# Adaptive-norm decoder kernel: the first modulation vectors summed on TensorE with a held condition column

## The chip, the cores and the metric

The kernel runs on one core of one Trainium2 chip. A core has a matrix engine (TensorE, "PE" in the profile, with its weight loads listed apart as "PEld"), a vector engine (VectorE, "DVE"), a scalar engine (ScalarE, "ACT"), a general engine (GpSimd, "POOL") and SyncE ("SP"), which here only issues DMA transfers. Each engine works through its own instructions in the order in which the program gives them, and waits on semaphores for the others. The metric is device microseconds of one execution, the median of several runs.

## The reference

Two decoder layers over 256 tokens of width 2048, everything in float32: layer 0 mixes tokens by gated linear attention, layer 1 by softmax attention with a forget gate, and each has a gated MLP with a short convolution. What matters here is the conditioning. Every sub-layer's input is a normalised x, scaled and shifted by vectors that one matrix-vector product makes from the condition c:

```
cond = jax.nn.silu(c)
mod = (cond @ w_mod[i] + b_mod[i])[:, None, :]
sh_m, sc_m, g_m, sh_f, sc_f, g_f = jnp.split(mod, 6, axis=-1)
h = rmsnorm(x, norm_mix[i]) * (1.0 + sc_m) + sh_m
```

Each of the six pieces has 2048 entries, so each needs a 2048 x 2048 float32 block of `w_mod` (16 MB) that is used once. The first mixer of layer 0 cannot start before it has the parts of `sc_m` and `sh_m` that its first input rows need.

## The kernel before

A 2048-wide vector is held as 16 columns of 128 partitions (k-tiles); `cT` holds the condition so, one column for each k-tile. The first projection of layer 0 (`gla`, lines 669 to 709) runs over the first 8 k-tiles of h for all its output columns, and then over the other 8 (`BLOCKS = (8, 8)`, line 41). So at the start only the first 1024 entries of `sc_m` and of `sh_m` are needed: 2 x 2048 rows x 1024 columns, 16 MB. The rest of the modulation is computed later, in the background of the matmuls, by the same function `mod_tasks` (line 228) with smaller tiles.

At the start `queue_norm` (line 1202) makes 8 tasks for `sc_m` and then 8 for `sh_m`, each with one load of 1 MB on SP's queue (line 242; two k-tiles of 128 x 1024, into a slot of the pool `big`, which has 12 slots of 8 KB a partition). For the first four k-tiles (`DIRECT = 4`) TensorE multiplies: the weights are the stationary operand, 128 x 128 at a time, and one column of `cT` moves (line 257). For the other twelve VectorE multiplies a whole 128 x 1024 tile by one number for each partition and adds it to an accumulator (lines 261 and 263). What is then still to be summed over the 128 partitions is turned by eight TensorE transposes into PSUM (line 285) and reduced along the free axis by VectorE (line 289); bias, the TensorE part and, for `sc_m`, the norm's gain follow on VectorE (lines 297 to 302).

Between the first task and the others the kernel loads x (`load_x`, line 407: two loads of 1 MB behind the first four weight loads, 32 transposes, copies and squares on ScalarE, sums of squares on VectorE), sums the squares over the partitions by a matmul (line 458) and computes the reciprocal root (`token_rstd`, line 465). `make_h` (line 486) then makes h of one k-tile at a time: VectorE multiplies x by the root (line 500, `hn`), ScalarE applies scale and shift and rounds (line 501), VectorE makes the low part (lines 502 and 503). The projection's weight tiles are split into a rounded high part on ScalarE (line 115) and a low part on VectorE (line 119); the low parts of the first tiles stand behind h of the second k-tile by an explicit order (`gate`, lines 504 and 563 to 569). The first four projection tiles are loaded behind the last of the 16 weight loads (`after_startup`, line 221).

The order on each engine's queue is written when the kernel is built, by a planner that simulates the run and takes, at each engine, what is ready, in program order of priority; `issue_after` adds fixed orders. The order of the planner is not in the source.

Of the kernel before, what the change touches and what calls it, by code (L numbers as in the profile page):

```python
# [9 lines left out]
F32 = mybir.dt.float32  # L10
# [7 lines left out]
P = 128  # L18
# [11 lines left out]
SECT = {"sh_m": 0, "sc_m": 1, "g_m": 2, "sh_f": 3, "sc_f": 4, "g_f": 5}  # L30
RING = 7
AHEAD = 3
DIRECT = 4
XAFTER = 1
WIDE = 4
SLOAD = 12
BACK = 1
# [31 lines left out]
def kernel(  # L69
# [21 lines left out]
    def nm(s):  # L91
        cnt[0] += 1
        return f"{s}_{cnt[0]}"

    def bigt(shape, s="big"):
        return big.tile(shape, F32, tag="s8", name=nm(s))

    def ringt(shape, s="w"):
        return ring.tile(shape, F32, tag="w", name=nm(s))
# [22 lines left out]
    def misc():  # L122
        return psM.tile([P, 512], F32, tag="m" if PS[1] else "a", name=nm("pm"))
# [97 lines left out]
    def after_startup(on=True):  # L221
        es = ExitStack()
        if on and startup["left"] > 0 and len(startup["loads"]) >= BACK:
            startup["left"] -= 1
            es.enter_context(tc.issue_after(startup["loads"][-BACK]))
        return es

    def mod_tasks(l, key, f0=0, fn=D, wide=False, direct=0, defer=False):


        s = SECT[key]
        width = fn // -(-fn // 1024)
        per = 1
        while 2 * per * width <= (2048 if wide else 1024):
            per *= 2

        def chunk(c0, kt, st):
            def load():
                st[kt] = bigt([P, per, width], "wm") if wide else ringt([P, per, width], "wm")
                src = w_mod[l, kt * P:(kt + per) * P, s * D + c0:s * D + c0 + width]  # L240
                with after_startup(not wide):
                    dma = nc.sync.dma_start(out=st[kt], in_=src.rearrange("(k p) m -> p k m", p=P))
                if wide:
                    startup["loads"].append(dma.ins)

            def f():
                wt = st.pop(kt)
                m0, mn = c0 // P, width // P
                last = kt + per == KT
                if direct and kt == 0:  # L250
                    st["p"] = psA.tile([P, 512], F32, tag="a", name=nm("pd"))
                for j in range(per):
                    k = kt + j
                    col = cT[:, k:k + 1]
                    if k < direct:
                        for m in range(mn):
                            nc.tensor.matmul(st["p"][:, m:m + 1], wt[:, j, m * P:(m + 1) * P], col,
                                             start=(k == 0 and m == 0), stop=(k == direct - 1), skip_group_check=True)
                    elif k == direct:
                        st["a"] = accp.tile([P, 1024], F32, tag="acc", name=nm("acc"))[:, :width]  # L260
                        nc.vector.tensor_scalar(out=st["a"], in0=wt[:, j, :], scalar1=col, scalar2=None, op0=ALU.mult)
                    else:
                        nc.vector.scalar_tensor_tensor(out=st["a"], in0=wt[:, j, :], scalar=col, in1=st["a"],  # L263
                                                       op0=ALU.mult, op1=ALU.add)
                if last and defer:
                    deferred.append(finish)
                elif last and wide:
                    finish()
                elif last:
                    resting.append([REST, finish])  # L270

            def finish():
                m0, mn = c0 // P, width // P
                if defer:
                    pt = psA.tile([P, 512], F32, tag="a", name=nm("pt"))
                    for m in range(mn):
                        nc.tensor.matmul(pt[:, m:m + 1], st["a"][:, m * P:(m + 1) * P], one, start=(m == 0),
                                         stop=(m == mn - 1), skip_group_check=True)
                    red = pt
                else:  # L280
                    red = tmp.tile([P, 8], F32, tag="red", name=nm("red"))
                for q0 in range(0, 0 if defer else mn, 4):
                    pt = psA.tile([P, 512], F32, tag="a", name=nm("pt")) if wide else misc()
                    for m in range(min(4, mn - q0)):
                        nc.tensor.transpose(pt[:, m * P:(m + 1) * P], st["a"][:, (q0 + m) * P:(q0 + m + 1) * P],  # L285
                                            ident)
                    if wide:
                        mq = min(4, mn - q0)
                        nc.vector.tensor_reduce(out=red[:, q0:q0 + mq], in_=pt[:, :mq * P]
                                                .rearrange("p (m k) -> p m k", k=P), axis=AX.X, op=ALU.add)  # L290
                        continue
                    for m in range(min(4, mn - q0)):
                        blk = pt[:, m * P:(m + 1) * P]
                        nc.scalar.activation(blk, blk, AF.Copy, accum_out=red[:, q0 + m:q0 + m + 1])
                dst = mod[:, l * 6 + s, m0:m0 + mn]
                b0 = l * 96 + s * KT + m0
                nc.vector.tensor_tensor(out=dst, in0=red[:, :mn], in1=bm[:, b0:b0 + mn], op=ALU.add)
                if direct:
                    nc.vector.tensor_tensor(out=dst, in0=dst, in1=st["p"][:, :mn], op=ALU.add)
                if key[:2] == "sc":  # L300
                    gsrc = r0["nmix" if key == "sc_m" else "nffn"] + l * KT + m0
                    nc.vector.scalar_tensor_tensor(out=dst, in0=dst, scalar=1.0, in1=vec[:, gsrc:gsrc + mn],
                                                   op0=ALU.add, op1=ALU.mult)
                elif key[0] == "g":
                    nc.vector.tensor_scalar_add(dst, dst, 1.0)
            return load, f
        tasks = []
        for c0 in range(f0, f0 + fn, width):
            st = {}
            for kt in range(0, KT, per):  # L310
                tasks.append(chunk(c0, kt, st))
        return tasks
# [18 lines left out]
    def bg_step():  # L331
        prefetch(2)
        if pending:
            pending.popleft()()
# [868 lines left out]
        queue(mod_tasks(0, "sc_m", f0 * P, nb * P, *kind))  # L1203
        queue(mod_tasks(0, "sh_m", f0 * P, nb * P, *kind))

    def drain_startup():
        while bg or pending:
            prefetch(WIDE)
            bg_step()

    queue_norm(0, BLOCKS[0], True, DIRECT)
    for _ in range(XAFTER):
        prefetch(WIDE)
        bg_step()
    load_x()
    first_h = make_h(0, "m")
    drain_startup()
    bounds = [sum(BLOCKS[:i]) for i in range(len(BLOCKS))]

    def staged_h(m):  # L1220
# [87 lines left out]
```

## Time and profile before

| What | Value |
|---|---|
| Timed runs, median (lowest to highest of 3) | 2458.89 us (2458.03 to 2460.32) |
| Span of the profiled execution | 2463.1 us |
| PE busy | 2407.8 us, 98% |
| DVE busy | 1896.1 us, 77% |
| ACT busy | 1283.7 us, 52% |
| DMA, mean over the span | 259 GB/s, 78% busy |
| HBM read | 633.14 MB |

The profile is one execution, and a separate one from the timed runs; its own time is its span, 2463.1 us from the first instruction to the last, 4.2 us above the median of the timed runs. Busy shares are means over the whole run; the change touches only the first 60 us or so, so the parts of the profile that matter are those of that stretch. "L257" is line 257 of the kernel. A float32 matmul that is not of the rounded kind appears in the trace as two PE instructions. The ends of matmuls are modelled, so the pace of a row of matmuls is read from its starts: the time of the whole row divided by the number in it. PEclk is the clock that the throttle granted to TensorE, as a share of full speed.

### The profile page before, as it was taken

What the parts mean: (1) busy time and instruction counts of PE and PEld (TensorE: products, weight loads), DVE (VectorE), ACT (ScalarE), POOL (GpSimd) and SP (SyncE); (2) the same over time, 40 slices, a digit from 0 to 9 for tenths busy, and PEclk for the clock granted to TensorE, in tenths of its full rate; (3) what the DMA queues carried; (4) which work ended last, traced back from release to release, by engine and by line L of the source; (5) the groups of instructions that cost most, each with busy time, mean ns of one, the idle gap of its engine ahead of it and who ended that gap; (6) DMA issues with size and microseconds to landing.
All of it is one profiled execution on the core that took longest, in us unless ns stands there. A gap on an engine that the chain in (4) does not pass through costs nothing.

```text
span 2463.1 us, 47142 instructions
## 1 busy us (share of the span) xinstructions
PE 2407.8 (98%) x19190; PEld 2322.5 (94%) x19190; DVE 1896.1 (77%) x2508; ACT 1283.7 (52%) x1908; POOL 13.1 (1%) x35
## 2 busy tenths in 40 slices
PE   6999999899999999999999999999999999999998
PEld 6988899899999999999988888999999999999998
DVE  6776989877789999977587888887876777767544
ACT  2446555454656666543454555554655555565433
POOL 0000000000000000000000000000000000000000
PEclk7999999999999999999999999999999999999999
DMA  9897878898668899899589887687677777756553
GB/s 369 273 310 234 295 266 304 285 318 305 211 193 275 302 316 305 300 315 319 181 273 314 302 281 238 217 293 254 214 237 230 232 236 237 228 193 219 192 189 112
DMA packets 184310, 638.33 MB, mean 259 GB/s; under 512 B 23961, under 2 KB 24971, under 8 KB 183708
## 3 DMA queue, kind: packets, MB, share of 16 engines
q1 hardware_dynamic: 183128, 634.12, 77.4%
q8 instruction: 150, 2.46, 0.4%
q10 hardware_dynamic: 964, 1.20, 0.1%
q14 instruction: 68, 0.56, 0.1%
HBM read 633.14 MB, written 2.10 MB: 258 GB/s over the span
## 4 chain that ended last, share of the span: by engine, by line
PE 87%; DMA 6%; DVE 5%; issue 2%; ACT 1%; SPq 0%; DVEq 0%; ACTq 0%
PE pa L587 23%; PE pa L586 23%; PE pa L585 23%; DMA wm<-in_w_mod_dram 6%; PE pa L621 4%; PE pa L623 4%; PE pa L622 4%; DVE wl L119 2%; DVE acc L263 1%; PE pm L285 1%; PE pm L458 0%; PE pm L825 0%; PE pm L1036 0%; PE pm L847 0%; PE pm L982 0%
## 5 line engine op out<-in xcount | busy, mean ns | idle before, releaser
L115 ACT CAST wh<-w 128x1024 fp32r<-128x1024 f32 x819 | 855.9, 1048 | 949.1 <-PE pa L586 660.5
L119 DVE TENSOR_TENSOR wl<-w,wh 128x1024 fp32r<-128x1024 f32 x819 | 993.3, 1219 | 338.6 <-ACT wh L115 332.4
L585 PE MATMUL pa<-h,wh 128*128 128x256 f32 x3584 | 990.4, 278 | 6.7 <-ACT h L501 6.2
L587 PE MATMUL pa<-h,wl 128*128 128x256 f32 x3584 | 991.3, 278 | 4.4 <-DVE wl L119 4.4
L586 PE MATMUL pa<-h,wh 128*128 128x256 f32 x3584 | 993.1, 278 | 0.5 <-DVE h L503 0.2
L587 PEld LDWEIGHTS pa<-h,wl 128*128 128x128 f32 x3584 | 675.3, 189 | 7.5 <-DVE wl L119 5.1
L585 PEld LDWEIGHTS pa<-h,wh 128*128 128x128 f32 x3584 | 674.6, 189 | 7.8 <-ACT h L501 6.9
L586 PEld LDWEIGHTS pa<-h,wh 128*128 128x128 f32 x3584 | 676.9, 189 | 1.5 <-DVE h L503 1.3
L263 DVE SCALAR_TENSOR_TENSOR acc<-wm,cT,acc 128x1024 f32<-128x1024 f32 x352 | 451.2, 1282 | 144.8 <-DMA wm<-in_w_mod_dram 143.3
L586 PE MATMUL pa<-op,wh 128*128 128x256 f32 x1920 | 528.1, 276 | 0.3 <-DVE op L519 0.3
L585 PE MATMUL pa<-op,wh 128*128 128x256 f32 x1920 | 527.7, 276 | 0.4 <-DVE xT L644 0.4
L587 PE MATMUL pa<-op,wl 128*128 128x256 f32 x1920 | 524.7, 276 | 0.5 <-DVE wl L119 0.5
L586 PEld LDWEIGHTS pa<-op,wh 128*128 128x128 f32 x1920 | 360.4, 188 | 0.5 <-DVE op L519 0.5
L585 PEld LDWEIGHTS pa<-op,wh 128*128 128x128 f32 x1920 | 359.8, 188 | 0.6 <-DVE xT L644 0.6
L587 PEld LDWEIGHTS pa<-op,wl 128*128 128x128 f32 x1920 | 358.0, 188 | 0.9 <-DVE wl L119 0.9
L622 PE MATMUL pa<-wh,h 128*128 128x512 f32 x512 | 201.8, 395 | 0.0
L621 PE MATMUL pa<-wh,h 128*128 128x512 f32 x512 | 199.7, 394 | 0.0
L623 PE MATMUL pa<-wl,h 128*128 128x512 f32 x512 | 194.5, 394 | 0.0
L621 PEld LDWEIGHTS pa<-wh,h 128*128 128x128 f32 x512 | 96.8, 189 | 19.7 <-issue 0.2
L623 PEld LDWEIGHTS pa<-wl,h 128*128 128x128 f32 x512 | 96.5, 189 | 20.0 <-DVE wl L119 0.7
L622 PEld LDWEIGHTS pa<-wh,h 128*128 128x128 f32 x512 | 96.7, 189 | 19.4
L1088 ACT ACTIVATE y<-u,cw 128x256 f32<-128x256 f32 x176 | 101.6, 599 | 23.4 <-DVE act L1104 21.1
(250 smaller groups left out, 1365.4 us busy)
## 6 DMA issues: line engine op xcount, KB each, us to landing
wm<-in_w_mod_dram SPq DMA_DIRECT2D x352, 512.0 KB, 5.2
w<-in_ffn_w_up_dram SPq DMA_DIRECT2D x320, 512.0 KB, 4.5
w<-in_ffn_w_down_dram SPq DMA_DIRECT2D x176, 512.0 KB, 4.5
w<-in_fox_w_in_dram SPq DMA_DIRECT2D x128, 512.0 KB, 5.0
w<-in_gla_w_in_dram SPq DMA_DIRECT2D x96, 512.0 KB, 5.2
wm<-in_w_mod_dram SPq DMA_DIRECT2D x16, 1024.0 KB, 12.4
w<-in_gla_w_out_dram SPq DMA_DIRECT2D x32, 512.0 KB, 6.1
w<-in_ffn_w_up_dram SPq DMA_DIRECT2D x64, 256.0 KB, 4.0
```

Source lines behind the costliest of these rows:

```text
L115: nc.scalar.copy(out=hi, in_=src)
L119: order["v"] = nc.vector.tensor_tensor(out=lo, in0=src, in1=hi.bitcast(F32), op=ALU.subtract).ins
L263: nc.vector.scalar_tensor_tensor(out=st["a"], in0=wt[:, j, :], scalar=col, in1=st["a"], op0=ALU.mult, op1=ALU.add)
L285: nc.tensor.transpose(pt[:, m * P:(m + 1) * P], st["a"][:, (q0 + m) * P:(q0 + m + 1) * P], ident)
L585: nc.tensor.matmul(o, wh[:, ms], rh, start=(first and m % 2 == 0), stop=False, skip_group_check=True)
L586: nc.tensor.matmul(o, wh[:, ms], rl, start=False, stop=False, skip_group_check=True)
L587: nc.tensor.matmul(o, wl[:, ms], rh, start=False, stop=last, skip_group_check=True)
L621: nc.tensor.matmul(o, lh[:, ts_], wh[:, hs_], start=first, stop=False)
L622: nc.tensor.matmul(o, ll[:, ts_], wh[:, hs_], start=False, stop=False)
L623: nc.tensor.matmul(o, lh[:, ts_], wl[:, hs_], start=False, stop=last)
L1088: nc.scalar.activation(y, u, AF.Identity, scale=cw[:, l * 3 + 2, r:r + 1], bias=cw[:, 6 + l, r:r + 1])
```

## The change

The tasks of the first 16 MB leave `mod_tasks`, which loses its `wide` and `direct` ways. In their place:

- A tile `cz` (128 x 16 x 32) from the pool `big` is zeroed on GpSimd, and the condition columns are copied to its column 0 for each k-tile. A small tile `halfsel` (128 x 2) gets four ones: rows 0 and 64 in column 0, rows 32 and 96 in column 1.
- The loads are the same 16 of 1 MB, in the same order on SP, four ahead of x and then always four ahead of the sum that uses them.
- For each load TensorE does four float32 matmuls. Now `cz` of a k-tile is stationary (128 x 32, one real column) and 512 weight columns move past it. The four go to the four groups of 32 output partitions of one PSUM bank: groups 0 and 1 take the two halves of the first k-tile of the pair, groups 2 and 3 those of the second. All eight loads of `sc_m` (then of `sh_m`) accumulate in that bank, and rows 0, 32, 64 and 96 of it hold the result.
- `early_finish` copies the bank to SBUF on ScalarE, and four float32 matmuls turn it: 128 columns of the copy are stationary, `halfsel` moves, so that the two k-tile rows of each half are added and come out as columns. One VectorE instruction adds the bias; for `sc_m` a second one applies the gain.
- VectorE has no part in the sums of these 16 MB any more. The background sums of all later modulation are as before.

```diff
-    queue_norm(0, BLOCKS[0], True, DIRECT)
-    for _ in range(XAFTER):
-        prefetch(WIDE)
-        bg_step()
+    cz = bigt([P, KT, 32], "cz")
+    nc.gpsimd.memset(cz, 0.0)
+    nc.gpsimd.tensor_copy(out=cz[:, :, 0:1], in_=cT.rearrange("p (k o) -> p k o", o=1))
+    halfsel = const.tile([P, 2], F32, name="halfsel")
+    nc.gpsimd.memset(halfsel, 0.0)
+    for g in range(4):
+        nc.gpsimd.memset(halfsel[32 * g:32 * g + 1, g % 2:g % 2 + 1], 1.0)
+    early = {}
+
+    def early_load(key, j):
+        early[key, j] = wt = bigt([P, 2, 1024], "wm")
+        c0 = SECT[key] * D
+        src = w_mod[0, 2 * j * P:(2 * j + 2) * P, c0:c0 + 1024]
+        startup["loads"].append(nc.sync.dma_start(out=wt, in_=src.rearrange("(k p) m -> p k m", p=P)).ins)
+
+    def early_sum(key, j):
+        wt = early.pop((key, j))
+        if j == 0:
+            early[key] = psA.tile([P, 512], F32, tag="a", name=nm("pe"))
+        for g in range(4):
+            nc.tensor.matmul(early[key][32 * g:32 * g + 32, :], cz[:, 2 * j + g // 2, :],
+                             wt[:, g // 2, (g % 2) * 512:(g % 2 + 1) * 512], start=(j == 0), stop=(j == KT // 2 - 1),
+                             skip_group_check=True)
+
+    def early_finish(key):
+        rows_ = t2("er")
+        nc.scalar.copy(out=rows_, in_=early.pop(key))
+        pt = misc()
+        for b in range(4):
+            nc.tensor.matmul(pt[:, 2 * b:2 * b + 2], rows_[:, b * P:(b + 1) * P], halfsel, start=(b == 0),
+                             stop=(b == 3), skip_group_check=True)
+        dst = mod[:, SECT[key], 0:8]
+        b0 = SECT[key] * KT
+        nc.vector.tensor_tensor(out=dst.rearrange("p (h b) -> p h b", h=2),
+                                in0=pt[:, 0:8].rearrange("p (b h) -> p h b", h=2),
+                                in1=bm[:, b0:b0 + 8].rearrange("p (h b) -> p h b", h=2), op=ALU.add)
+        if key == "sc_m":
+            nc.vector.scalar_tensor_tensor(out=dst, in0=dst, scalar=1.0, in1=vec[:, r0["nmix"]:r0["nmix"] + 8],
+                                           op0=ALU.add, op1=ALU.mult)
+
+    todo = [(key, j) for key in ("sc_m", "sh_m") for j in range(KT // 2)]
+    for key_j in todo[:WIDE]:
+        early_load(*key_j)
     load_x()
     first_h = make_h(0, "m")
-    drain_startup()
+    for i, (key, j) in enumerate(todo):
+        if i + WIDE < len(todo):
+            early_load(*todo[i + WIDE])
+        early_sum(key, j)
+        if j == KT // 2 - 1:
+            early_finish(key)
```

More of the change, by code (lines that the diff above doesn't have):

```diff
@@ L226, in after_startup, with mod_tasks @@
         return es
-    def mod_tasks(l, key, f0=0, fn=D, wide=False, direct=0, defer=False):
+    def mod_tasks(l, key, f0=0, fn=D, defer=False):
         s = SECT[key]
@@ L233, in mod_tasks @@
         per = 1
-        while 2 * per * width <= (2048 if wide else 1024):
+        while 2 * per * width <= 1024:
             per *= 2
@@ L238, in load @@
             def load():
-                st[kt] = bigt([P, per, width], "wm") if wide else ringt([P, per, width], "wm")
+                st[kt] = ringt([P, per, width], "wm")
                 src = w_mod[l, kt * P:(kt + per) * P, s * D + c0:s * D + c0 + width]
[L241 to L244, printed above, removed]
+                with after_startup():
+                    nc.sync.dma_start(out=st[kt], in_=src.rearrange("(k p) m -> p k m", p=P))
             def f():
                 wt = st.pop(kt)
-                m0, mn = c0 // P, width // P
                 last = kt + per == KT
-                if direct and kt == 0:
-                    st["p"] = psA.tile([P, 512], F32, tag="a", name=nm("pd"))
                 for j in range(per):
@@ L254, in f @@
                     col = cT[:, k:k + 1]
[L255 to L259, printed above, removed]
+                    if k == 0:
                         st["a"] = accp.tile([P, 1024], F32, tag="acc", name=nm("acc"))[:, :width]
@@ L266, in f @@
                     deferred.append(finish)
-                elif last and wide:
-                    finish()
                 elif last:
@@ L274, in finish @@
                 if defer:
-                    pt = psA.tile([P, 512], F32, tag="a", name=nm("pt"))
+                    red = psA.tile([P, 512], F32, tag="a", name=nm("pt"))
                     for m in range(mn):
-                        nc.tensor.matmul(pt[:, m:m + 1], st["a"][:, m * P:(m + 1) * P], one, start=(m == 0),
+                        nc.tensor.matmul(red[:, m:m + 1], st["a"][:, m * P:(m + 1) * P], one, start=(m == 0),
                                          stop=(m == mn - 1), skip_group_check=True)
-                    red = pt
                 else:
@@ L282, in finish @@
                 for q0 in range(0, 0 if defer else mn, 4):
-                    pt = psA.tile([P, 512], F32, tag="a", name=nm("pt")) if wide else misc()
+                    pt = misc()
                     for m in range(min(4, mn - q0)):
@@ L286, in finish @@
                                             ident)
[L287 to L291, printed above, removed]
                     for m in range(min(4, mn - q0)):
@@ L297, in finish @@
                 nc.vector.tensor_tensor(out=dst, in0=red[:, :mn], in1=bm[:, b0:b0 + mn], op=ALU.add)
-                if direct:
-                    nc.vector.tensor_tensor(out=dst, in0=dst, in1=st["p"][:, :mn], op=ALU.add)
                 if key[:2] == "sc":
@@ new lines, in early_finish @@
+    def early_finish(key):
+        rows_ = t2("er")
+        nc.scalar.copy(out=rows_, in_=early.pop(key))
+        pt = misc()
+        for b in range(4):
[9 more added lines that the diff above has]
+                                           op0=ALU.add, op1=ALU.mult)
```

6 lines of the change are left out of this document (removed).

## The prediction

> **What bounds the kernel now.** I read the page first, then the busy time in two equal stretches, and then the chain of work that ended last, in order of time. (Columns of the stretches: stretch; length; busy time and instructions of PE, PEld, DVE, ACT, POOL; PEclk; DMA share; GB/s.)
>
> ```profile
> span 2463.1 us, 47142 instructions
> ...
> 0.00:61.60 61.60, 39.76 (x183) 37.15 (x184) 42.38 (x65) 14.91 (x24) 1.19 (x9) 0.78 0.93 369
> 61.60:123.20 61.60, 60.37 (x458) 57.89 (x458) 46.72 (x61) 30.06 (x38) 0.00 (x0) 0.95 0.83 273
> ```
>
> After the first 61.6 us TensorE hardly rests (60.4 of 61.6 us), and it goes on so to the end. So the start is a stretch ahead of a TensorE-bound kernel: one microsecond less until the first projection is one microsecond less at the end, as long as the work behind it moves along as a whole. It does: the next weight loads are released by the split of the first tiles, not by the clock on the wall.
>
> What ends the start is seen in the chain and in the timelines of the engines:
>
> ```profile
> 1.26 2.15 SPq L242 DMA_DIRECT2D wm<-in_w_mod_dram  x4
> 6.46 2.96 SPq L411 DMA_DIRECT2D xtok<-in_x_dram  x2
> ...
> 22.23 13.12 SPq L242 DMA_DIRECT2D wm<-in_w_mod_dram  x6
> 36.16 6.39 SPq L554 DMA_DIRECT2D w<-in_gla_w_in_dram  x4
> ```
>
> ```profile
> 42.00:51.00 9.00, 9.00 (x43) 8.82 (x42) 8.33 (x12) 0.47 (x1) 0.00 (x0) 0.50 1.03 409
> 59.50:64.60 5.10, 2.13 (x8) 1.84 (x8) 4.33 (x11) 3.99 (x7) 0.00 (x0) 0.50 0.01 2
> ```
>
> ```profile
> 52.19 5.23 DVE L263 SCALAR_TENSOR_TENSOR acc<-wm,cT,acc 128x1024 f32<-128x1024 f32 x4
> 52.81 1.04 ACT L115 CAST wh<-w 128x1024 fp32r<-128x1024 f32 x1 [9.53 <-DMA w<-in_gla_w_in_dram]
> 54.09 1.04 ACT L115 CAST wh<-w 128x1024 fp32r<-128x1024 f32 x1 [0.23 <-DMA w<-in_gla_w_in_dram]
> 57.48 1.97 PE L285 MATMUL pt<-ident,acc 128*128 128x128 f32 x8 [5.96 <-DVE acc L263]
> 59.48 0.69 DVE L289 TENSOR_REDUCE red<-pt 128x4 f32<-128x512 f32 x1 [0.16 <-PE pt L285]
> 60.21 0.17 DVE L297 TENSOR_TENSOR mod<-red,bm 128x8 f32<-128x8 f32 x1
> 60.61 1.58 ACT L501 ACTIVATE h<-hn,mod 128x256 fp32r<-128x256 f32 x3 [5.47 <-DVE mod L299]
> 64.62 0.58 PE L587 MATMUL pa<-h,wl 128*128 128x256 f32 x1 [1.23 <-DVE wl L119]
> ```
>
> The DMA engines are full (409 GB/s), so 1 MB (1.049 million bytes) takes 2.56 us. The order on SP is 4 weight loads, x, 12 weight loads, then the projection's tiles of 0.5 MB. The first of these had landed when its cast began, at 52.81. Half a megabyte is 1.28 us, so the sixteenth load landed at about 52.8 - 1.3 = 51.5. That is the floor of this start. VectorE is behind it: it runs four sums in a row until 57.42, then come transposes, reduction and bias, and h starts at 60.61. So there are 9.1 us between the last landing and h, 5.9 of them VectorE's backlog, 3.2 the turn.
>
> **The change, part by part.** *Removed*: VectorE's 24 passes and TensorE's 32 matmuls with one moving column. *Unchanged*: the sixteen loads, their order, x between them, and so the floor of 51.5. One slot of the pool is taken by `cz`, so 11 instead of 12 are left. The last loads were issued at 35 and landed 16 us later. An issue that comes a few us late is still in time; without that lead every late us would be one us. x's sums are in before 42.81 now, their root at 49.7:
>
> ```profile
> 42.81 0.47 ACT L467 ACTIVATE rb<-pm,epsc 128x256 f32<-128x256 f32 x1 [9.22 <-PE pm L458]
> 49.31 0.42 DVE L474 SCALAR_TENSOR_TENSOR rb<-ra,rb 128x256 f32<-128x256 f32 x1
> ```
>
> These 6.9 us are a few short operations with VectorE's sums between them; without the sums they shorten, so x has some 8 us to spare. `cz` and `halfsel` are small GpSimd fills, on an engine that does nothing there.
>
> *Added, a sum.* Each load brings four float32 matmuls, eight PE instructions, 512 columns each. For their price I take the projection's gate, which has the same form with fewer rows, and for the clock a row of transposes before and after the throttle let go:
>
> ```profile
> 228.89 1.98 PE L724 MATMUL pm<-wg,aT 17*128 17x512 f32 x4
> 21.43 1.07 PE L416 MATMUL pm<-ident,xtok 128*128 128x128 f32 x4
> 28.79 1.14 PE L416 MATMUL pm<-ident,xtok 128*128 128x128 f32 x8 [0.82 <-ACT xT L418]
> ```
>
> Four transposes took as long as eight did later, so full clock is twice half clock (PEclk reads 1.00 in both places, since it shows no event before 27.2; I go by the pace). Four gate instructions in 1.98 us, of which the last one's tail is some 0.2, start about 0.43 apart at full clock, so 0.86 at half. Eight in series would be 3.4 or 6.9 us for a load that arrives every 2.56: TensorE would become the bound. Side by side in four column groups they are two passes, 0.9 or 1.7 us, and the DMA stays the bound. No row here has four groups, but the scores of the gated attention go to two groups of 64. The loop (lines 817 to 826) issues all 16 instructions of one block of rows, then all of the next:
>
> ```profile
> 292.44 0.69 PE L825 MATMUL pm<-q,kend 128*64 128x64 f32 x9
> 292.91 0.27 PE L825 MATMUL pm<-q,k 128*64 128x64 f32 x1
> 292.97 0.22 PE L825 MATMUL pm<-q,kend 128*64 128x64 f32 x1
> 293.02 0.22 PE L825 MATMUL pm<-q,k 128*64 128x64 f32 x1
> 293.02 0.22 PE L825 MATMUL pm<-q,kend 128*64 128x64 f32 x1
> 293.08 0.22 PE L825 MATMUL pm<-q,k 128*64 128x64 f32 x1
> 293.08 0.22 PE L825 MATMUL pm<-q,kend 128*64 128x64 f32 x1
> ```
>
> Nine in one group start (0.69 - 0.22)/8 = 0.059 apart. Where the second block begins (`q,k` at 292.91) both groups run at that pace at once, and the new group starts while three older instructions of the other are still to start. With such a look-ahead all four groups of the change should be open together. I take two passes for the sum; the upper end is eight.
>
> The Trainium skill, "TensorE: Matmul & The Clock Gate", Part 3, says the reverse on the order: matmuls are strictly first in, first out, in start and in end. By that rule the second pass of each group would hold the next group back, a load would take five passes instead of two, and the result is the second rival below. The rows at 292.9 speak against it: a younger matmul starts before three older ones.
>
> *The clock.*
>
> ```profile
> 23.80:27.20 3.40, 3.38 (x15) 2.75 (x16) 3.36 (x4) 2.26 (x5) 0.00 (x0) 1.00 1.02 408
> 34.00:37.40 3.40, 2.15 (x11) 2.15 (x11) 3.30 (x5) 0.00 (x0) 0.23 (x2) 0.50 1.03 411
> 64.70:68.10 3.40, 3.40 (x16) 3.40 (x17) 3.40 (x5) 0.92 (x2) 0.00 (x0) 0.50 0.70 202
> 133.00:136.40 3.40, 1.46 (x7) 0.88 (x5) 0.94 (x1) 2.30 (x4) 0.00 (x0) 1.00 1.00 369
> 136.40:139.80 3.40, 3.00 (x11) 2.76 (x12) 3.40 (x5) 1.36 (x9) 0.00 (x0) 0.50 0.67 230
> ```
>
> A stretch of 3.4 us with PE busy for 1.46 was followed by half clock, one busy throughout by full clock. The sums keep PE busy for about 1.0 of 2.56 us at full clock (39%, like 1.46 of 3.4) and 1.8 (70%) at half. So I take half clock at the end of the start, as now. The same page, Part 1, asks only that no gap between bursts exceeds some 3 us; by that the clock would stay up, and h would come as in the second rival. The row at 133 speaks against: no gap there was that long, and the clock fell.
>
> *Added, the finish.* Copy of 128 x 512 out of PSUM; eight PE instructions with 128-column weights and two moving columns; one addition (0.17, as L297).
>
> ```profile
> 22.53 0.59 ACT L418 COPY xT<-pm 128x512 f32<-128x512 f32 x1 [16.22 <-PE pm L416]
> 36.80 4.82 PEld L257 LDWEIGHTS pd<-cT,wm 128*128 128x128 f32 x22
> ```
>
> Copy 0.6; turn 8 x 0.22 = 1.8, with its tail 1.9; addition with its hand-over 0.2.
>
> *A wait that is new.* The copy stands on ScalarE, where the casts of the first two projection tiles run from 52.81 and from 54.09. The planner writes the order. If only the first is ahead of the copy, the copy starts at 53.85; if both are, at 55.13. Nothing in the trace tells which (it has no such copy), so I take the middle. Behind the copy wait the turn, the addition, h and the whole projection.
>
> *The sum.* Landing 51.5; two passes and tail 2.0, to 53.5; copy at 53.85 or 55.13, done 54.45 or 55.7; turn to 56.35 or 57.6; addition to 56.55 or 57.8. Against 60.61 that is 4.0 or 2.8 us; the middle is 3.4. What follows h (the first low parts on VectorE, 64.62 - 60.61 = 4.0 us until TensorE is fed) keeps its order. In the profiled execution 2463.1 - 3.4 = 2459.7; against the median, 2458.9 - 3.4 = 2455.5. The 15 us of VectorE that fall away in the second half of the start were hidden or were this backlog; nothing else is worth time.
>
> **The rivals.** 1: *The four groups run in series.* Then TensorE decides, from the point where a sum takes over 2.56 us: fewer than 1.35 groups at once at full clock. 16 x 3.4 = 55 us from 7, with 2 us more for the first sums at half clock and some 5 for x's transposes and sums: about 69, copy 0.6, turn 0.9 and addition 0.2 at full clock, h at 70.7, 10 later than now; the first projection tile at full clock gives 2 back. 2458.9 + 8 = 2467. For it: no row has a 32-wide group or four at once. Against it: the rows at 292.9.
>
> 2: *Full clock at the end of the start*, by partial overlap that keeps TensorE busy. With five passes, a load takes 2.15 of 2.56 us (84%) and the clock stays up; with two passes it could be raised by a busy stretch. The end of the sum moves by little (51.5 + 2.4 = 53.9 in the first case), the turn shrinks by 0.9, and the projection starts at full clock. Now it runs from 64.62 to 68.2 at half pace, which costs 1.8. With a copy at 53.9 to 55.1: h at 55.6 to 56.9, 3.7 to 5.0 earlier, and 1.8 on top: 5.5 to 6.8, so about 2452.8. For it: the stretch from 23.8 to 27.2, busy for 3.38 of 3.40 with x's transposes, did lift the clock. Against it: 70% is well short of that.
>
> 3: *The gain does not arrive.* The planner puts the sum over x's squares behind the late sums on TensorE's queue (in the old trace it already waits for 22 one-column matmuls), or late slots open a hole in the DMA queue. If the square sum is behind the sixteenth sum, it starts at 53.5, and root and `hn` need about 4.5 more (42.81 to 49.31 now, with sums in between): h at 58 to 60. Time 2457 to 2459.
>
> **How the numbers follow.** Less than 0.2% (4.9 us) can't be told from no change here. Forecast (gain 2.8 to 4.0, half clock) 0.48; rival 2 0.27; rival 3 0.13; rival 1, with other losses of its kind, 0.12. Rival 2 is above that, and so is 0.04 of the forecast, if the hand-overs are shorter than I take them: faster 0.31. The rest of the forecast (0.44) and rival 3 are the same, 0.57; slower 0.12. The forecast's own range is 2454.5 to 2457. The range reaches to rival 2 with the lower end of its copy and to rival 3 with a small loss: 2451 to 2461; rival 1 is left out.
>
> **What would show it.** Two passes: PE matmuls into the new bank start in pairs of groups or all four within 0.2 us, and a load's eight take about 1.9 us. The floor: the cast of the first projection tile still starts near 52.8; if it comes later, slots were late. The finish: copy between 53.6 and 55.2, h between 56 and 58 instead of 60.61. The clock: half until some 3.5 us after the projection starts, else rival 2. The prediction is wrong if the last sum ends later than 56, or if the stretch from h on changes its length by more than 2 us.

## The result, and the profile after

The changed kernel takes 2542.89 us (median of 4 runs, 2542.28 to 2544.96), the kernel before, beside it on the same chip, 2459.61 us (2458.03 to 2462.13). The ratio is 1.0334, with a 95% interval of 1.0322 to 1.0346: slower by 3.3%, 83 us more. The profiled execution has a span of 2543.2 us.

The start did what was forecast. The timeline of the changed kernel around the last sums (start, length, engine, line, operation, number of instructions, idle time before it; L1205 is the new sum, L1211 the copy, L1214 the turn, L480 h, L566 the projection's low part, L587 before):

```profile
46.37 1.94 PE L1205 MATMUL pe<-wm,cz 128*32 128x512 f32 x8 [0.62 <-DMA wm<-in_w_mod_dram]
48.93 1.74 PE L1205 MATMUL pe<-wm,cz 128*32 128x512 f32 x8 [0.62 <-DMA wm<-in_w_mod_dram]
51.49 1.06 PE L1205 MATMUL pe<-wm,cz 128*32 128x512 f32 x8 [0.82 <-DMA wm<-in_w_mod_dram]
52.74 1.04 ACT L113 CAST wh<-w 128x1024 fp32r<-128x1024 f32 x1 [15.95 <-DMA w<-in_gla_w_in_dram]
53.70 0.58 ACT L1211 COPY er<-pe 128x512 f32<-128x512 f32 x1
54.17 1.05 ACT L113 CAST wh<-w 128x1024 fp32r<-128x1024 f32 x1
54.33 1.87 PE L1214 MATMUL pm<-halfsel,er 128*128 128x2 f32 x8 [1.77 <-ACT er L1211]
56.23 0.17 DVE L1218 TENSOR_TENSOR mod<-pm,bm 128x8 f32<-128x8 f32 x1 [15.69 <-PE pm L1214]
56.43 1.58 ACT L480 ACTIVATE h<-hn,mod 128x256 fp32r<-128x256 f32 x3 [1.21 <-DVE mod L1218]
60.45 0.58 PE L566 MATMUL pa<-h,wl 128*128 128x256 f32 x1 [1.23 <-DVE wl L117]
```

h starts at 56.43, 4.2 us ahead of the 60.61 of before, and the first low part at 60.45 instead of 64.62. So the loss is all behind this place: from h to the end it is 2463.1 - 60.61 = 2402.5 us before and 2543.2 - 56.43 = 2486.8 after, 84.3 more.

There the work is the same, but slower. The page of the changed kernel (busy time; chain of work that ended last; the largest groups, with busy time and mean ns of one; a 512-column group, from the groups by line):

```profile
span 2543.2 us, 47116 instructions
...
PE 2495.0 (98%) x19190; PEld 2384.0 (94%) x19190; DVE 1875.1 (74%) x2478; ACT 1286.2 (51%) x1910; POOL 14.1 (1%) x42
...
PE 96%; DMA 2%; DVE 1%; ACT 0%; issue 0%; SPq 0%; DVEq 0%
...
L564 PE MATMUL pa<-h,wh 128*128 128x256 f32 x3584 | 1011.1, 284 | 5.4 <-ACT h L480 5.3
...
L564 PE MATMUL pa<-op,wh 128*128 128x256 f32 x1920 | 538.9, 282 | 0.0
...
L601 PE MATMUL pa<-wh,h 128*128 128x512 f32 x512 | 204.3, 400 | 0.0
```

The same lines of the kernel before (L585 there is L564 here, L622 is L601):

```profile
PE 87%; DMA 6%; DVE 5%; issue 2%; ACT 1%; SPq 0%; DVEq 0%; ACTq 0%
...
L585 PE MATMUL pa<-h,wh 128*128 128x256 f32 x3584 | 990.4, 278 | 6.7 <-ACT h L501 6.2
...
L585 PE MATMUL pa<-op,wh 128*128 128x256 f32 x1920 | 527.7, 276 | 0.4 <-DVE xT L644 0.4
...
L622 PE MATMUL pa<-wh,h 128*128 128x512 f32 x512 | 201.8, 395 | 0.0
```

Each matmul is about 6 ns longer, with the same operands and shape. Ends are modelled, so the pace is better read from starts. A stretch of 50 us in the middle of both, first before, then after (after the length: busy time and number of PE, PEld, DVE, ACT, POOL; clock; DMA share; GB/s):

```profile
2000.00:2050.00 50.00, 50.00 (x443) 50.00 (x443) 37.28 (x49) 27.23 (x36) 0.00 (x0) 1.00 0.75 236
```

```profile
2000.00:2050.00 50.00, 50.00 (x422) 50.00 (x422) 29.97 (x39) 31.23 (x59) 0.00 (x0) 1.00 0.68 221
```

TensorE never rests in either, the clock is full in both, but 422 matmuls fit where 443 did: 118.5 instead of 112.9 ns each, about 5% slower. From start to start over the whole trace, the 256-column matmuls of the rounded kind went from 113.4 to 119.1 ns, the 512-column ones from 227.4 to 233.4. Each of the three products has 3584 + 1920 of the first and 512 of the second: 16,512 x 5.7 ns = 94 us and 1,536 x 6.0 ns = 9 us, 103 us together. The net loss behind h is 84 us. Part of the other 19 is found in the two traces: from h to the end TensorE is idle for 26.3 us instead of 34.1, and busy at half clock for 24.1 us instead of 37.0, which is worth some 6 us. A slower TensorE waits less (the chain of before ran over DMA and DVE for 6% and 5%, that of after for 2% and 1%); the half clock is partly chance, since an execution of the kernel before with one unused constant added (the first experiment below) has 24.9 us of it at the old pace. Some 5 us stay unexplained. The plain float32 matmuls, two instructions each, kept their pace (215 ns for 256 columns, 109 for 128, in both).

### The profile page after: what moved, and what is told of

Its sections match the earlier page's. It is cut to its first block, busy times and chain, and to the rows that moved or that the text cites. A ratio compares the mean times of both kernels' runs of the same rounds, so it can differ in the third digit from the quotient of the medians.

```text
span 2543.2 us, 47116 instructions
## 1 busy us (share of the span) xinstructions
PE 2495.0 (98%) x19190; PEld 2384.0 (94%) x19190; DVE 1875.1 (74%) x2478; ACT 1286.2 (51%) x1910; POOL 14.1 (1%) x42
## 4 chain that ended last, share of the span: by engine, by line
PE 96%; DMA 2%; DVE 1%; ACT 0%; issue 0%; SPq 0%; DVEq 0%
PE pa L565 26%; PE pa L566 26%; PE pa L564 26%; PE pa L600 5%; PE pa L601 5%; PE pa L602 5%; DMA wm<-in_w_mod_dram 1%; DMA w<-in_gla_w_in_dram 1%; PE pm L271 1%; DMA xtok<-in_x_dram 0%; PE pm L804 0%; PE pm L1015 0%; PE pm L826 0%; PE pm L961 0%; PE pm L979 0%; PE pm L437 0%
## 5 line engine op out<-in xcount | busy, mean ns | idle before, releaser
L564 PE MATMUL pa<-h,wh 128*128 128x256 f32 x3584 | 1011.1, 284 | 5.4 <-ACT h L480 5.3
L565 PE MATMUL pa<-h,wh 128*128 128x256 f32 x3584 | 1015.5, 284 | 0.8 <-DVE h L482 0.6
L566 PE MATMUL pa<-h,wl 128*128 128x256 f32 x3584 | 1011.9, 284 | 1.2 <-DVE wl L117 1.2
L564 PEld LDWEIGHTS pa<-h,wh 128*128 128x128 f32 x3584 | 680.3, 190 | 6.2 <-ACT h L480 5.6
L566 PEld LDWEIGHTS pa<-h,wl 128*128 128x128 f32 x3584 | 680.5, 190 | 4.1 <-issue 2.3
L565 PE MATMUL pa<-op,wh 128*128 128x256 f32 x1920 | 540.2, 282 | 0.0
L564 PE MATMUL pa<-op,wh 128*128 128x256 f32 x1920 | 538.9, 282 | 0.0
L566 PE MATMUL pa<-op,wl 128*128 128x256 f32 x1920 | 535.5, 282 | 0.0
L252 DVE SCALAR_TENSOR_TENSOR acc<-wm,cT,acc 128x1024 f32<-128x1024 f32 x330 | 422.7, 1281 | 104.5 <-DMA wm<-in_w_mod_dram 103.3
L564 PEld LDWEIGHTS pa<-op,wh 128*128 128x128 f32 x1920 | 363.1, 189 | 0.0
L566 PEld LDWEIGHTS pa<-op,wl 128*128 128x128 f32 x1920 | 361.0, 189 | 0.0
L601 PE MATMUL pa<-wh,h 128*128 128x512 f32 x512 | 204.3, 400 | 0.0
L600 PE MATMUL pa<-wh,h 128*128 128x512 f32 x512 | 202.3, 399 | 0.0
L601 PEld LDWEIGHTS pa<-wh,h 128*128 128x128 f32 x512 | 96.7, 189 | 21.9
```

The costliest lines, as they stand in the source:

```text
L564: nc.tensor.matmul(o, wh[:, ms], rh, start=(first and m % 2 == 0), stop=False, skip_group_check=True)
L565: nc.tensor.matmul(o, wh[:, ms], rl, start=False, stop=False, skip_group_check=True)
L566: nc.tensor.matmul(o, wl[:, ms], rh, start=False, stop=last, skip_group_check=True)
L600: nc.tensor.matmul(o, lh[:, ts_], wh[:, hs_], start=first, stop=False)
L601: nc.tensor.matmul(o, ll[:, ts_], wh[:, hs_], start=False, stop=False)
```

## The experiments

What could slow every rounded matmul by 6 ns, when the change ends at 57 us? It puts one small constant (`halfsel`, 32 bytes a partition) ahead of all later tiles, so that everything behind it lies 32 bytes higher. And it takes away the early use of another small tile: `red` (line 281, two slots, 64 bytes a partition), which `finish` took at the start in the kernel before. The addresses of the two programs show that the pools place a kind of tile where it is first taken. In the kernel before, `red` came ahead of the split weight tiles `wh` and `wl`; in the changed one they come first, 64 bytes lower. The addresses in the two programs, bytes a partition:

```
          big (h)      wh       wl      red    wh+64 - big   wl+192 - big
before     53952   178112   195520   178048   124224         141760
after      53984   178080   195488   214432   124160         141696
```

The 64 and 192 are `HELD = (16, 48)`, columns by which `split_w` (line 112) shifts a stationary high and low part inside its tile. The slots are steps of 4352 = 17 x 256, the parts of h lie multiples of 1024 apart, so a distance from the moving h to the loaded weights, modulo 256, holds for nearly all pairs: 64 (high) and 192 (low) before, 0 and 128 after. In the 512-column matmuls, where the weights move, h is loaded and `HELD` is not used, the distance from the moving weights to h is 0 before and 64 after. Theory A is that the absolute place counts, theory D that this distance does; the expectations below name the others.

**The constant alone, and the change without it.** To the kernel before a constant of the same size is added, and nothing reads it:

```diff
     xT = const.tile([P, KT, T], F32, name="xT")
+    shim = const.tile([P, 2], F32, name="shim")
+    nc.gpsimd.memset(shim, 0.0)
```

> The kernel before, with one unused constant of 8 bytes a partition put behind the last constant (it takes 32 bytes), and nothing else. Theory A, the place in SBUF: the changed kernel's small constant moved every tile that TensorE reads for the projections from a multiple of 64 bytes to 32 bytes past one, and each rounded matmul pays some 5 ns for that. Then this kernel is as slow behind the start: matmuls with 256 columns start 118 to 119 ns apart instead of 113, and the time is 2459.6 + about 87 = 2545 to 2549 us. Theory B, the 32-wide column groups leave TensorE in a slower way of working: no such group here, so 113 ns and 2459.6 us. Theory C, the program's length or instruction order: 2459.6 us, since TensorE's instructions are the same.

In the changed kernel, `halfsel` moves into spare columns of `cz`:

```diff
-    cz = bigt([P, KT, 32], "cz")
+    czt = bigt([P, KT * 32 + 2], "cz")
+    cz = czt[:, :KT * 32].rearrange("p (k o) -> p k o", o=32)
-    halfsel = const.tile([P, 2], F32, name="halfsel")
+    halfsel = czt[:, KT * 32:KT * 32 + 2]
```

> The changed kernel with its two selection columns kept behind the condition columns in the same pool slot, so that no constant is added and the tiles stand at multiples of 64 bytes again. Theory A: 113 ns a matmul, and the start of the changed kernel (h at 56.4 instead of 60.6): 2459.6 - 4.2 = 2455.4 us, between 2453.5 and 2457. Theories B and C: 118 to 119 ns, 2543 us as the changed kernel.

Measured: the constant costs nothing, 2460.08 us, ratio 1.0 (0.9989 to 1.0011); without it the change is as slow, 2540.8 us, 1.0327 (1.031 to 1.0344). The same stretch, first with the constant, then without it:

```profile
2000.00:2050.00 50.00, 50.00 (x444) 50.00 (x442) 37.04 (x48) 27.29 (x37) 0.00 (x0) 1.00 0.75 233
```

```profile
2000.00:2050.00 50.00, 50.00 (x422) 50.00 (x421) 33.04 (x41) 29.62 (x54) 0.00 (x0) 1.00 0.67 211
```

Theory A falls twice. In the first all tiles moved together and the pace stayed; in the second all tiles are back at multiples of 64, yet the weights are still 64 bytes closer to h, as `red` is still missing ahead of them.

**The distance alone, in the kernel before.** Nothing of the change; only `HELD`:

```diff
-HELD = (16, 48)
+HELD = (24, 56)
```

> The kernel before with the stationary weight tiles alone moved on by 32 bytes (offsets 24 and 56 columns instead of 16 and 48); h, the moving operand, stays at a multiple of 64. Theory A1, a moving row off the 64-byte grid costs one more line: 113 ns, 2459.6 us. Theory A2, a stationary tile off the grid costs it: 118 to 119 ns for the 256-column matmuls, unchanged 227 ns for the 512-column ones (these use no offset), about 2459.6 + 16500 x 5.3 ns = 2547 us less a little.

and with the constant of above and the weights 32 bytes lower:

```diff
-HELD = (16, 48)
+HELD = (8, 40)
```

> The kernel before with the 8-byte constant of the first run and the weight offsets set back by 32 bytes (8 and 40 columns), so that the stationary weights of the 256-column matmuls are at multiples of 64 and their moving operand h is 32 past. Theory A1 (moving): 118 to 119 ns, 2545 to 2549 us. Theory A2 (stationary): 113 ns for the 256-column matmuls, 232 for the 512-column ones, where both are off; 2459.6 + 1536 x 5.8 ns = 2468 us.

2520.19 us (ratio 1.0245, 1.022 to 1.0271) and 2528.34 us (1.0278, 1.0254 to 1.0303). Eight columns of shift in either direction cost 60 to 70 us. Theory A1 gave the first run 113 ns and theory A2 the second; both ran at about 118, so both fall. Neither run gives the full loss, so two more go to exactly the distance of the changed kernel, one by the weights alone:

```diff
-HELD = (16, 48)
+HELD = (0, 32)
```

> The kernel before with one constant changed: weight offsets 0 and 32 columns instead of 16 and 48, so the stationary weights stand 64 bytes lower and nothing else moves, which is what the change did to the 256-column matmuls. Theory D: 119 ns for the 256-column matmuls, 227 for the 512-column ones: what the changed kernel lost, less the 512-column matmuls' share of 9 us, so 2459.6 + 87 - 9 = about 2537 us. Theory B, or any theory that needs the column groups: 2459.6 us.

the other with h, and all behind it, 64 bytes higher, and the weights held where they were by the same `HELD`:

```diff
-HELD = (16, 48)
+HELD = (0, 32)
...
+    gapp = ctx.enter_context(tc.tile_pool(name="gapp", bufs=1))
     big = ctx.enter_context(tc.tile_pool(name="big", bufs=NBIG))
...
+    nc.gpsimd.memset(gapp.tile([P, 16], F32, name="gap"), 0.0)
```

> The kernel before with 64 bytes put between the pool of the raw weights and the pool that holds h, and the weight offsets lowered by 64 bytes (0 and 32 columns): the stationary weights keep their addresses and their distance from the raw weights, h stands 64 bytes higher. Theory D (distance from h): 119 ns for the 256-column matmuls, 227 for the 512-column ones, 2459.6 + about 16300 x 5.6 ns = 2548, less what waits absorb: 2530 to 2550 us. Theory E, the distance from the raw weights that ScalarE and VectorE read at the same time: 113 ns, 2459.6 us.

2537.04 us (1.0318, 1.03 to 1.0336) and 2538.68 us (1.0325, 1.0307 to 1.0343). The stretch and a group with the weights lower, then the stretch with h higher:

```profile
2000.00:2050.00 50.00, 50.00 (x422) 50.00 (x421) 33.50 (x40) 27.08 (x38) 0.00 (x0) 1.00 0.70 222
```

```profile
L585 PE MATMUL pa<-h,wh 128*128 128x256 f32 x3584 | 1008.9, 283 | 6.8 <-ACT h L501 6.2
```

```profile
2000.00:2050.00 50.00, 50.00 (x422) 50.00 (x421) 33.38 (x40) 27.18 (x38) 0.00 (x0) 1.00 0.71 221
```

The kernel before, with no part of the change in it, shows the changed kernel's pace to the instruction, whichever of the two operands moved, and the first experiment kept its pace with both moved. So it counts how the two lie to each other. Theories B (column groups) and C (program length or order) fall with the lowered weights, where nothing but their places differs from the kernel before; theory E falls with the raised h, since the raw weights kept their distance from the split ones.

A rival is left: tiles behind h moved with it, so the pace might hang on what VectorE, ScalarE and GpSimd read or write meanwhile. The traces speak against it. Where all three rest from 0.3 us before a 256-column matmul starts until 0.3 us after the next one does, the pace is the same as elsewhere: 113.5 ns in the kernel before (232 such places), 118.9 in the changed one (113 places). The DMA engines are not shut out in this way.

**The change with the distance mended.** First in the changed kernel by its shift:

```diff
-HELD = (16, 48)
+HELD = (32, 64)
```

> The changed kernel as it is, with the weight offsets moved on by 64 bytes (32 and 64 columns instead of 16 and 48). In the changed kernel the little tile of the reductions is first used after the weight tiles, so the pool gives the weight tiles places 64 bytes lower against h than before; this puts the stationary weights back to the old distance from h, while the 512-column matmuls (no offset) stay 64 bytes off. Theory D, the distance between the tile that is loaded as weights and the tile that moves decides the pace: 113 ns for the 256-column matmuls, 233 for the 512-column ones; 2459.6 - 4.2 + 1536 x 5.9 ns = 2464 us. Theory B, column groups leave TensorE slow: 119 ns, 2543 us.

2465.17 us, ratio 1.0025 (1.0014 to 1.0035). The 256-column matmuls are back at 113.5; the 512-column ones stay at 233.3, since there the weights move and have no `HELD`. Then by giving all tiles their old order, with one fill behind the first `make_h`:

```diff
     first_h = make_h(0, "m")
+    nc.vector.memset(tmp.tile([P, 8], F32, tag="red", name=nm("red")), 0.0)
```

> The changed kernel with one more line: a tile of the reductions' tag is taken and zeroed behind the first make_h, where the kernel before first took it, so the pool gives the weight tiles their old distance from h (all tiles stand 32 bytes higher than before, which the first run showed to cost nothing). Theory D: 113 and 227 ns as before, and the changed start: 2459.6 - 4.2 = 2455.4 us, between 2453 and 2457, faster than both kernels. Theory B: 119 ns, 2543 us.

2456.59 us against 2457.94 us, ratio 0.9988 (0.9979 to 0.9997): the change with the old places is faster than the kernel before by 2.9 us (0.7 to 5.2) of the forecast 3.4, just clear of the noise (the two medians lie 1.35 us apart). Its stretch, its chain and its start:

```profile
2000.00:2050.00 50.00, 50.00 (x443) 50.00 (x443) 36.40 (x46) 27.63 (x37) 0.00 (x0) 1.00 0.74 234
```

```profile
PE 86%; DMA 7%; DVE 4%; issue 1%; ACT 1%; DVEq 0%; SPq 0%; ACTq 0%
```

```profile
53.86 0.58 ACT L1211 COPY er<-pe 128x512 f32<-128x512 f32 x1
...
56.59 0.60 ACT L480 ACTIVATE h<-hn,mod 128x256 fp32r<-128x256 f32 x1 [1.22 <-DVE mod L1218]
...
60.61 0.58 PE L566 MATMUL pa<-h,wl 128*128 128x256 f32 x1 [1.23 <-DVE wl L117]
```

That it is 8.6 us below the experiment with `HELD = (32, 64)` fits the 9 us that the 512-column matmuls were reckoned at.

**Which of the two parts.** Low or high part alone at the slow distance, in the kernel before. The low part:

```diff
-HELD = (16, 48)
+HELD = (16, 32)
```

> The kernel before with only the low parts of the weights 64 bytes lower (offsets 16 and 32 columns). Theory D1, a load of weights disturbs the row that moves while it runs, and only that pair's distance counts: one interval in three is long, the one in which the low part is loaded (from the high-by-low matmul to the low-by-high one), 119 against 113, and the time is 2458 + 26 = 2484 us. Theory D2, a matmul's own weights against its own moving row: the interval behind the low-by-high matmul is the long one, the same time. Theory D3, the whole set of places decides at once: all three long or none.

The high part:

```diff
-HELD = (16, 48)
+HELD = (0, 48)
```

> The kernel before with only the high parts 64 bytes lower (offsets 0 and 48 columns). Theory D1: the two intervals in which a high part is loaded are long (from high-by-high to high-by-low, and from low-by-high to the next high-by-high), the third stays at 113; 2458 + 52 = 2510 us. Theory D2: the two intervals behind the matmuls with the high part are long, the same time. Theory D3: all three long, or none.

2522.24 us (1.026, 1.024 to 1.028) and 2516.44 us (1.0237, 1.0216 to 1.0258). Either part alone brings over two thirds of the 79 us of both, and the two don't add up: 65 + 59 us would be 124. With only the low part moved, theories D1 and D2 expected one long step in three; two of the three steps between matmuls slow to 119.0 and 119.5 ns and the third to 116.2, so both fall there. With only the high part the steps are 119.0, 119.4 and 115.0. That is near D2, which expected the first two to be long and 2510 us, and against D1, which had the first and the third. D3, all three long or none, holds in neither, as the third step is shorter. Four more pairs, in the kernel before, look for a rule, in this order:

```diff
-HELD = (16, 48)
+HELD = (48, 16)
...
+HELD = (32, 64)
...
+HELD = (16, 16)
...
+HELD = (48, 48)
```

> The kernel before with the two offsets exchanged (48 and 16 columns): distances from h of 192 bytes for the high part and 64 for the low part, modulo 256. Rule 1, each part at 64 modulo 128: 113 ns, 2458 us. Rule 2, the parts 128 apart and on these two places: 113 ns. Rule 3, only the old pair: 119 ns, about 2537 us.

> The kernel before with both parts 64 bytes higher (32 and 64 columns): distances 128 and 0. Rule 1: 119 ns, 2537 us, as with 64 bytes lower. A rule with a period of 256 in which only 0 and 128 in that order are slow: 113 ns, 2458 us.

> The kernel before with both offsets at 16 columns: distances 64 and 64. Rule 1: 113 ns, 2458 us. Rule 2 (the parts must be 128 apart): slower, 2480 to 2540 us.

> The kernel before with both offsets at 48 columns: distances 192 and 192. Rule 1: 113 ns, 2458 us. Rule 2: slower, 2480 to 2540 us.

All that was measured, by distance (bytes modulo 256, high and low part), with the three paces between one matmul and the next in ns (from high-by-high to high-by-low, on to low-by-high, and back to high-by-high; one number where they agree):

| Distance | Kernel | Time, us | Ratio (95% interval) | Paces |
|---|---|---|---|---|
| 64 / 192 | before with the constant | 2460.08 | 1.0 (0.9989 to 1.0011) | 113.4 |
| 192 / 64 | before, `HELD` (48, 16) | 2481.78 | 1.0102 (1.005 to 1.0154) | 114.8, 116.1, 114.9 |
| 64 / 64 | before, (16, 16) | 2478.72 | 1.0075 (1.0053 to 1.0097) | 114.7 |
| 192 / 192 | before, (48, 48) | 2517.97 | 1.0236 (1.0197 to 1.0276) | 117.9, 117.8, 117.7 |
| 0 / 192 | before, (0, 48) | 2516.44 | 1.0237 (1.0216 to 1.0258) | 119.0, 119.4, 115.0 |
| 64 / 128 | before, (16, 32) | 2522.24 | 1.026 (1.024 to 1.028) | 119.0, 119.5, 116.2 |
| 96 / 224 | before, (24, 56) | 2520.19 | 1.0245 (1.022 to 1.0271) | 118.9, 118.8, 116.1 |
| 128 / 0 | before, (32, 64) | 2526.16 | 1.027 (1.0234 to 1.0305) | 119.4, 117.6, 118.1 |
| 32 / 160 | before with the constant, (8, 40) | 2528.34 | 1.0278 (1.0254 to 1.0303) | 118.0, 118.8, 118.3 |
| 0 / 128 | before, (0, 32) | 2537.04 | 1.0318 (1.03 to 1.0336) | 119.1 |

The clean pair is the one that the kernel before has. That each part need only lie at 64 modulo 128 (rule 1) was refuted: 192 / 192 meets that and costs 2.4%. Rules 2 and 3 gave 192 / 64 a pace of 113 and of 119 ns, and it has neither as a mean.

The paces of 114.7 to 116.1 ns at 192 / 64 and 64 / 64 are mixtures of two. The same 50 us as above, first with `HELD = (48, 16)`, then with `(16, 16)`:

```profile
2000.00:2050.00 50.00, 50.00 (x444) 50.00 (x443) 36.20 (x46) 26.17 (x34) 0.00 (x0) 1.00 0.75 238
```

```profile
2000.00:2050.00 50.00, 50.00 (x427) 50.00 (x427) 35.85 (x46) 26.73 (x36) 0.00 (x0) 1.00 0.72 221
```

From 1850 to 1900 us it is the other way round, 423 matmuls in the first and 444 in the second. At these two distances an uninterrupted row of matmuls, often hundreds long, runs at one of the two paces, and the pace changes mostly where a row is interrupted (in the second trace, 31 of 34 changes). About a third of the matmuls is slow in each, which also explains why the times of these two kernels spread from 2469 to 2499 us. So the distance alone does not set the pace there; what tips a row no run shows.

**The order on ScalarE.** To the kernel with the old places, the copy goes ahead of the casts (`order["r"]` is what the first casts are ordered behind):

```diff
-        nc.scalar.copy(out=rows_, in_=early.pop(key))
+        order["r"] = nc.scalar.copy(out=rows_, in_=early.pop(key)).ins
```

> The run with the old places, and the casts of the first projection tiles ordered behind the copy of the last sums (in the changed kernel the first cast ran from 52.74 to 53.78 while the sum had ended at 52.55, and the copy started at 53.70). If the copy is then on the path to h as the prediction had it: copy at 52.7, h at about 55.4 instead of 56.4, and 1 us off the end: 2454 to 2456 us, which the interval will hardly tell from the run with the old places; the profile will. If the casts are what h waits for, or the first low parts are: h earlier, but the first full matmuls of the projection at the same 64 as in the changed kernel, and no gain.

Beside the run with the old places the copy comes 0.71 us earlier, h 1.07:

```profile
53.15 0.58 ACT L1211 COPY er<-pe 128x512 f32<-128x512 f32 x1 [16.27 <-PE pe L1205]
...
55.52 1.58 ACT L480 ACTIVATE h<-hn,mod 128x256 fp32r<-128x256 f32 x3
...
59.54 0.58 PE L566 MATMUL pa<-h,wl 128*128 128x256 f32 x1 [1.24 <-DVE wl L117]
```

The 1.07 us are not the order's alone: in this execution the turn ran at full clock, 1.05 us instead of 1.87, and h, whose vector was ready at 55.04, then waited for the second cast. The time is 2454.99 us, ratio 0.9989 (0.9978 to 1.0), and the span 2451.3 beside 2451.6 us. One microsecond at the start can't be told at the end here.

**The sums without column groups.** In the kernel with the old places the condition column gets a 128-wide stationary tile, so that all four sums of a load go to the whole array, one behind the other:

```diff
-    cz = bigt([P, KT, 32], "cz")
...
+    czs = [bigt([P, 8, 224], "cz") for _ in range(2)]
...
-            nc.tensor.matmul(early[key][32 * g:32 * g + 32, :], cz[:, 2 * j + g // 2, :],
+            k = 2 * j + g // 2
+            nc.tensor.matmul(early[key], czs[k // 8][:, k % 8, 96 - 32 * g:224 - 32 * g],
```

> The run with the old places, with the column groups given up: the condition column stands in one of four columns of a 128-wide stationary tile that is zero otherwise, so each of the four matmuls of a load writes all 128 partitions and none can run beside another. The price of groups in series, the first rival of the prediction: eight passes of 0.43 us, 3.4 us for a load that arrives every 2.56, the last sum at about 69, h at 70 to 71 instead of 56.4, less 2 us for a clock that is up when the projection starts: 2456 + 12 = about 2468 us. If the groups were not what made the sums short: h at 56.4, 2456 us.

2470.15 us, ratio 1.0053 (1.0036 to 1.0069), h at 71.45:

```profile
27.15 3.60 PE L1207 MATMUL pe<-wm,cz 128*128 128x512 f32 x8
...
69.52 0.59 ACT L1213 COPY er<-pe 128x512 f32<-128x512 f32 x1 [4.55 <-PE pe L1207]
...
71.45 1.59 ACT L480 ACTIVATE h<-hn,mod 128x256 fp32r<-128x256 f32 x3 [1.34 <-DVE mod L1220]
```

Eight in series take 3.60 us at full clock, in four groups 1.06; in the last sum of the changed kernel the first passes of all four groups start within 0.02 us (from 51.486) and the second passes follow from 51.940. So the groups do run side by side, and this is what the change would cost if they didn't.

## Why the prediction was wrong

The forecast of 2455.5 us missed by 87 us, far outside its range, on a sign it gave 0.12.

- **The step that failed** is "as long as the work behind it moves along as a whole. It does", and with it "nothing else is worth time". The sum had terms for what instructions do, wait for and queue behind, and none for where their tiles lie. The text counted the slot that `cz` takes, but not that with VectorE's sums the first use of `red` falls away and 64 bytes of address with it. The missing term is 16,512 x 5.7 ns + 1,536 x 6.0 ns = 103 us, of which 84 arrived: 8 of the other 19 us are shorter waits and some 6 less time at half clock, the rest is open. The prediction's own test caught it: the stretch from h on was to keep its length within 2 us, and it grew by 84.
- **Rival 1**, the one slower case, was not what happened: no group waits for another. Its h was nearly right: forecast 70.7, measured 71.45 once the groups were really taken away. Its price was too low: 8 us forecast, 12.7 measured (2470.15 against 2457.43), as the 2 us that a full clock was to give back didn't come; the clock fell to half at 72.7, just behind h.
- **The floor** held: first projection cast forecast near 52.8, seen at 52.74; the last sum, which waited for the sixteenth load, began at 51.49 (51.5 worked out). The work that falls away was miscounted, without effect on the sum: TensorE's matmuls with one moving column are 64, not 32.
- **Two passes** held: a load's eight take 1.94 us at half clock (forecast 1.9) and 1.06 at full. By the first-in, first-out rule that the Trainium skill gives ("TensorE: Matmul & The Clock Gate", Part 3) five passes were to be expected; the trace does not agree.
- **The clock** was right in its place, not in its way. It was at half when h and the projection came, as forecast, but the last sum ran at full clock, in part as rival 2 had it. The sum allowed two passes and tail 2.0 us; they took 1.06. That is chance: with the old places the last sum took 1.94. The rule by busy time that the forecast used is not sound either: its own row from 42.00 to 51.00 has TensorE busy throughout, and the clock stayed at half. Nor did the rule of gaps hold that the prediction cites ("only" is its own word): the clock fell at 43.51 and at 53.75, with no gap above 1.8 us from 37 us on.
- **The copy** came between the two casts, at 53.70 (forecast 53.85 for that order). Turn 1.87 (1.9) and addition 0.17 were as worked out; h at 56.43 is just ahead of the 56.55 of the lower branch. Since the copy waited for the cast, the faster last sum brought nothing. The prediction had nothing to choose the order by and took the middle; that the earlier one came is luck.
- **Rival 3** did not occur: the sum over x's squares ran at 35.61, long before h.
- **The gain of the start** was right as far as it can be measured: with the old places, 2.9 us (0.7 to 5.2) against 3.4. The mechanism at the start was right, its size too within that wide interval, and a side effect thirty times larger hid it.

## What to carry to other kernels

Taking a tile out of a kernel, or using it later, can move other tiles, and with them the pace of matmuls that the change never touches. After any edit that adds, drops or reorders the first use of a tile, compare the addresses of the operands of the main matmuls, and their start-to-start pace in one undisturbed stretch, before any other explanation. A loss spread evenly over a stretch that the change doesn't reach is the mark; the cure here was one line that gives the tile its old place.

## What the runs showed of the hardware

**Pace and distance.** A rounded 256-column matmul with weights loaded for each takes 113.4 ns at one distance between the bytes of the moving and of the loaded operand, and 119.1 ns when the weights lie 64 bytes lower or h 64 bytes higher; a shift of both together by 32 bytes changes nothing. Of ten distances one was fast nearly throughout, seven were slow nearly throughout and cost 2.4% to 3.2% of the whole kernel, and two went back and forth and cost 0.8% and 1.0%. For the 512-column matmuls the fast distance was 0 (227.4 ns) and the slow one 64 (233.4). The Trainium skill ("TensorE: Matmul & The Clock Gate", Part 2, "Step-by-step: what each phase is for") says that TensorE has two read ports and that "Loading the next tile's weights doesn't steal SBUF read bandwidth from the running matmul." Here the running matmuls do depend on where the loaded weights lie, 422 instead of 443 matmuls in 50 us by a 64-byte shift of the weights alone, and the measurement decides. Why is open: a collision of the two reads in the memory would fit, but no run shows which pair of rows meets, and the table gives no simple rule. Nor is it known why the plain float32 matmuls are spared.

**A clock that toggles.** The changes of clock in this trace lie whole multiples of 3.41 us apart. The changed kernel in such steps (columns as above):

```profile
40.09:43.51 3.42, 1.52 (x12) 0.16 (x8) 0.45 (x2) 0.00 (x0) 0.00 (x0) 1.00 1.04 414
43.51:46.92 3.41, 2.49 (x12) 0.40 (x16) 0.00 (x0) 0.00 (x0) 0.00 (x0) 0.50 1.02 407
46.92:50.34 3.42, 2.79 (x16) 0.20 (x8) 0.00 (x0) 0.00 (x0) 0.00 (x0) 0.50 1.02 406
50.34:53.75 3.41, 1.39 (x12) 0.16 (x8) 0.00 (x0) 1.00 (x2) 0.00 (x0) 1.00 1.04 416
53.75:57.17 3.42, 1.95 (x9) 1.87 (x9) 0.27 (x2) 2.21 (x5) 0.24 (x2) 0.50 1.02 407
```

A step with TensorE busy for 1.52 of 3.42 us was followed by half clock. At half clock the same sums keep it busy for longer, and a step with 2.79 of 3.42 (82%) was followed by full clock, one with 2.49 (73%) was not. So a load that arrives at a steady rate made the clock swing here. These shares are no threshold: with the old places the clock stayed at half through steps of 78%, 73% and 74% from 48.96 us on and rose only at 66.02, and in the kernel before the clock stayed at half from 42 to 51 us with TensorE busy all the time. What the clock is at a given moment of the start differs from one execution to the next.
